# A state space layer as a scan pipeline over feature chunks, with its turn table and read-out operators made one stage earlier

## The chip, the cores and the metric

The kernel runs on one core of a Trainium2 chip. The metric is the device time of one execution in microseconds. TensorE (PE) multiplies matrices, with its weight loads (PEld) beside it; VectorE (DVE), ScalarE (ACT) and GpSimd (POOL) work on tiles in SBUF and read TensorE's results from PSUM; SyncE (SP) and the other queues issue transfers. Each engine runs its instructions in the order in which they stand in its queue.

## The reference

Two transformer blocks on 512 tokens of 1024 features in float32: a retention and pooling mixer, a mixture of 32 experts, a gated input, then a state space layer, a gated feed-forward net, a short convolution and a second feed-forward net. The change concerns the state space layer and the stage before it:

```python
h = h + sigmoid(rms_norm(h) @ ple_gate_w) * (p @ ple_proj_w)   # gated input
# state space layer: 64 groups of 16 features, 64 complex states each
lr, li, dt = minimum(a_re, -1e-4), a_im, exp(log_step)
abar = exp(lr * dt) * (cos(li * dt) + 1j * sin(li * dt))
u = modulate(rms_norm(x, norm1_g), sh1, sc1)                   # (512, 64 groups, 16)
state[t] = abar * state[t - 1] + bbar @ u[t]                   # by group, complex
y = real(c @ state) + d * u
val, gate = split(gelu(y) @ ssm_w_out)
x = x + g1 * val * sigmoid(gate)
```

## The kernel before

The program runs stage by stage: mixer, router and experts, `stage_ple` (gated input), `stage_s5` (state space layer), then feed-forward, convolution and feed-forward. A scheduler and tile pools turn the code into one queue of instructions per engine; tiles with one tag share slots, and an instruction that wants a slot waits until the slot's last readers are done. A product in float32 is done as three in a reduced format: a weight block is loaded (`raw`, `half`), ScalarE makes its high part (`wh`, L94), VectorE the rest (`wl`, L95), and TensorE multiplies three times (L115 to L117).

`stage_ple` multiplies the normalised input by `ple_gate`. The token factors come from a power on GpSimd (`lrstd`, L229), which TensorE spreads over the partitions (`bc`, L241). Each of the eight output blocks c is then evacuated: VectorE scales the product (`lg`, L1343), ScalarE takes the sigmoid (L1344), VectorE multiplies by the projected input `pj` (L1345), adds to `res` (L1346), and two sums of squares `lacc` collect on ScalarE and VectorE (L204, L220). Beside it run the last columns of a modulation vector: `halves` loads six `half` tiles on GpSimd's queue, VectorE reduces each (`adaj`, L1077). At the end GpSimd takes the roots `r2` (L1369) and `r1`.

`stage_s5` cuts the 512 tokens into 64 chunks of 8 steps. For each of eight feature chunks k it normalises (`zh`), regroups (`zt`, `zct`, `zu`, `zU`), and multiplies with operators made earlier (`s_pt`) to get the input that each chunk of 8 steps adds to the states (`zs`). The recurrence over the 64 chunks then runs on VectorE for all features at once, in two halves, one step after the other:

```python
nc.vector.tensor_tensor(t[:, j, :, :, :2], a8, x[:, c - 1]..., ALU.mult)              # L1518
net.scanned = nc.vector.tensor_reduce(x[:, c], t[:, j], AX.X, ALU.add).ins             # L1520
```

Here `a8` holds the complex factor of eight steps. ScalarE copies the states into `zxq` (L1524). TensorE adds the part within the chunks (`zy<-zT,zU`, L1562, all eight k before the recurrence is done) and the part from the states (`zy<-zQ,zxq`, L1573), turns the result back to features (`zf`, L1583); ScalarE applies the gelu (L1586), and ScalarE, VectorE and GpSimd split it in two (`zgah`, `zgal`, L1589 to L1592) for the output layer `ssm_out`, whose first product is `mm<-zgah,wh` (L146).

The read-out operators `zQ` are made in `readout`, called inside `stage_s5` and issued behind `r2`: sixteen times three products on GpSimd (L1117, L1119, L1121, tile `ro`), each written to DRAM (`q_d`) and loaded back by SyncE.

Of the kernel before, what the change touches and what calls it, by code (L numbers as in the profile page):

```python
# [22 lines left out]
S = 512  # L23
# [19 lines left out]
EXTRA = 0  # L43
NA = 5
ZK = (0, 5, NK)
# [468 lines left out]
def stage_mix_out(net, mixed, ps, moe):  # L514

    nc, a = net.nc, net.a
    with ExitStack() as es:
        net.h1 = net.h1p.tile([128, NT, D], F32, tag="big", name="h1")
        router = Router(net, es, moe)
        moe.prefetch(6)  # L520
# [12 lines left out]
        moe.prefetch(9)  # L533
# [243 lines left out]
class Moe:  # L777
# [30 lines left out]
    def prefetch(self, n):  # L808

        net = self.net  # L810
        while len(self.loaded) < n:
            j = len(self.loaded)
            nm, e, b = self.order[j]
            src = net.a[nm][e][b]
            q = j % (9 + EXTRA)
            if q < 6:
                t = net.load(src, self.raw2, "raw2")
            else:
                t = net.load(src) if q < 9 else net.load(src, self.raw3, "raw3")
            self.loaded.append(t)  # L820
# [76 lines left out]
    def experts(self, es):  # L897
# [6 lines left out]
        if EXTRA:  # L904
            self.raw3 = pool("raw3", EXTRA)
# [12 lines left out]

# [190 lines left out]
def powers4(t):  # L1109
    return t.rearrange("p (g t h) -> p g t h", g=GP, t=8)  # L1110


def power_product(eng, out, t, xr, xi, y1, y2, op):

    sh = [128, GP, 8, 16]
# [8 lines left out]
class S5Prepare:  # L1124


    def __init__(self, net, p1, pt):
# [5 lines left out]
        net.a8 = net.rt.tile([128, 2, G // 2, 2], F32, name="a8")  # L1133
# [4 lines left out]
    def units(self):  # L1138
# [24 lines left out]
        for b in range(2):  # L1163
# [8 lines left out]
            sincos(net, ang, ei, lam, t[:, :256], t[:, 256:])  # L1172
            tt(ei, er, ei, ALU.mult)
# [6 lines left out]

        for h in range(2):
            r = slice(64 * h, 64 * h + 64)
            for q in range(2):
                nc.vector.tensor_copy(net.a8[r, q, :, q], ar[r, 8, h::2])
            nc.vector.tensor_scalar(net.a8[r, 0, :, 1], ai[r, 8, h::2], -1.0, None, op0=ALU.mult)
            nc.vector.tensor_copy(net.a8[r, 1, :, 0], ai[r, 8, h::2])
# [83 lines left out]
def stage_ple(net):  # L1270
# [3 lines left out]
    with ExitStack() as es:  # L1274
# [22 lines left out]
        net.linear_fm(a["ple_proj"], 2, lambda k: pact[k], evac_p)  # L1297
        first = [net.load(a["ple_gate"][b]) for b in range(2)]
# [52 lines left out]
        for z in range(2):  # L1351
            t = net.op.tile([128, 32, 128], F32, tag="op", name=f"s_pt{z}")
            for q in range(2):
                o = slice((2 * z + q) * 2048, (2 * z + q + 1) * 2048)
                with tc.issue_after(copied[-1]):
                    nc.scalar.dma_start(t[:, 16 * q:16 * q + 16].rearrange("p g x -> p (g x)"), net.p_d[:, o])
# [60 lines left out]
def readout(net):  # L1417

    nc, a = net.nc, net.a
    e, w = [net.whp.tile([128, 2048], F32, tag="wh", name=f"ro{j}") for j in range(2)]  # L1420
# [506 lines left out]
```

## Time and profile before

| what | value |
|---|---|
| median of 3 runs | 2694.6 us (2694.42 to 2696.72) |
| profiled execution | 2704.24 us, its span 2701.8 us |
| TensorE busy | 2558.8 us, 95% of the span |
| VectorE busy | 1898.3 us, 70% |
| ScalarE busy | 1374.8 us, 51% |
| GpSimd busy | 430.1 us, 16% |
| granted TensorE clock, mean | 0.97 |

Busy shares are means over stages that differ; the windows among the rows below cut the span into stages. A row of a timeline gives the start in us from the span's beginning, the duration (of all that it groups, with x and their count), the engine, the line and the operation (out<-in), and in brackets the idle time before it and what ended that. A row of windows gives the engines in the order PE, PEld, DVE, ACT, POOL, with the number of instructions in brackets.

### The profile page before, as it was taken

The numbers are of one execution on the slowest core, as the hardware profiler recorded it, in microseconds if no ns is written. First come the engines' busy times: TensorE is split into PE (matmuls) and PEld (weight loads), VectorE is DVE, ScalarE is ACT, GpSimd is POOL, SyncE is SP. The second block draws the span as 40 slices with busy tenths as digits, with TensorE's granted clock in tenths as the row PEclk, the third lists the DMA queues.
The fourth block names the chain that finished last, engine by engine and source line by source line (L and its number), as shares of the span: only waits on it lengthen the run. The fifth ranks groups of instructions, "written<-read, shape, count | busy, mean of one in ns | idle before, by whom it ended". The sixth has DMA issues, their size and how long they took to land.

```text
span 2701.8 us, 31654 instructions
## 1 busy us (share of the span) xinstructions
PE 2558.8 (95%) x12270; PEld 1927.6 (71%) x12271; DVE 1898.3 (70%) x2410; ACT 1374.8 (51%) x1513; POOL 430.1 (16%) x252
## 2 busy tenths in 40 slices
PE   8999788999999999999999865999999999999998
PEld 6767555666666666666666755888788888888886
DVE  8974877999999999898988577775553544532333
ACT  7344565777777777777776644242122322322221
POOL 3362312031312112031200071000000000000000
PEclk9999898999999999999999987999999999999999
DMA  6435788999999999999996642754552222223221
GB/s 210 172 110 214 292 289 305 355 341 383 346 383 356 373 360 375 352 358 373 368 372 239 248 150 80 278 188 177 210 214 104 103 97 103 83 86 103 101 85 63
DMA packets 110432, 634.76 MB, mean 235 GB/s; under 512 B 16043, under 2 KB 21419, under 8 KB 43331
## 3 DMA queue, kind: packets, MB, share of 16 engines
q1 hardware_dynamic: 97971, 599.69, 59.6%
q0 software_dynamic: 11584, 28.27, 4.2%
q10 hardware_dynamic: 720, 4.72, 0.4%
q8 instruction: 98, 1.61, 0.2%
q14 instruction: 59, 0.48, 0.1%
HBM read 607.15 MB, written 28.61 MB: 235 GB/s over the span
## 4 chain that ended last, share of the span: by engine, by line
PE 66%; issue 18%; DMA 7%; DVE 6%; POOL 2%; ACT 2%; SPq 0%; POOLq 0%; DVEq 0%; ACTq 0%
PE gu L115 8%; PE gu L116 8%; PE gu L117 8%; PE mm L115 7%; PE mm L116 7%; PE mm L117 7%; PE dn L116 4%; PE dn L117 4%; PE dn L115 4%; DMA xg<-hn_d,tabim 2%; DMA acc_d<-y,tabim 2%; DMA raw<-in_w_ada 1%; PE mm L146 1%; DVE wl L95 1%; PE mm L147 1%
## 5 line engine op out<-in xcount | busy, mean ns | idle before, releaser
L95 DVE TENSOR_TENSOR el<-raw,eh 128x2048 fp32r<-128x2048 f32 (+1 forms) x396 | 874.5, 2221 | 99.3 <-ACT eh L94 93.2
L94 ACT ACTIVATE eh<-raw 128x2048 fp32r<-128x2048 f32 (+1 forms) x396 | 735.2, 1866 | 294.0 <-PE gu L117 209.9
L94 ACT ACTIVATE wh<-raw 128x1024 fp32r<-128x1024 f32 (+1 forms) x238 | 222.0, 981 | 478.2 <-PE mm L116 291.9
L116 PE MATMUL gu<-el,xh 128*88 128x512 f32 x1024 | 404.2, 395 | 0.0
L117 PE MATMUL gu<-eh,xl 128*88 128x512 f32 x1024 | 402.4, 393 | 0.0
L115 PE MATMUL gu<-eh,xh 128*88 128x512 f32 x1024 | 400.6, 397 | 0.0
L95 DVE TENSOR_TENSOR wl<-raw,wh 128x1024 fp32r<-128x1024 f32 (+1 forms) x238 | 265.5, 1148 | 79.9 <-ACT wh L94 79.6
L116 PE MATMUL mm<-nl,wh 128*128 128x512 f32 x816 | 318.3, 390 | 0.0
L115 PE MATMUL mm<-nh,wh 128*128 128x512 f32 x816 | 317.9, 390 | 0.0
L117 PE MATMUL mm<-nh,wl 128*128 128x512 f32 x816 | 316.8, 389 | 0.0
L117 PEld LDWEIGHTS gu<-eh,xl 128*88 128x88 f32 x1024 | 158.4, 155 | 78.4 <-issue 0.5
L116 PEld LDWEIGHTS gu<-el,xh 128*88 128x88 f32 x1024 | 158.9, 155 | 75.8 <-issue 0.5
L115 PEld LDWEIGHTS gu<-eh,xh 128*88 128x88 f32 x1024 | 158.3, 155 | 75.3 <-issue 0.3
L115 PE MATMUL dn<-eh,ath 128*88 128x512 f32 x512 | 204.0, 401 | 0.4
L116 PE MATMUL dn<-el,ath 128*88 128x512 f32 x512 | 202.5, 399 | 0.0
L117 PE MATMUL dn<-eh,atl 128*88 128x512 f32 x512 | 202.4, 396 | 0.0
L750 POOL DMA_INDIRECT acc_d<-y,tabim x32 | 93.8, 2931 | 633.0 <-ACT y L958 566.1
L744 POOL DMA_INDIRECT xg<-hn_d,tabim x32 | 142.2, 4444 | 318.9 <-PE xt L758 157.4
L115 PEld LDWEIGHTS mm<-nh,wh 128*128 128x128 f32 x816 | 153.2, 188 | 32.7
L117 PEld LDWEIGHTS mm<-nh,wl 128*128 128x128 f32 x816 | 153.2, 188 | 32.3
L116 PEld LDWEIGHTS mm<-nl,wh 128*128 128x128 f32 x816 | 153.2, 188 | 31.5
L1681 DVE TENSOR_TENSOR fs<-fs,mm 128x512 f32<-128x512 f32 x44 | 30.2, 687 | 205.8 <-PE mm L117 196.4
(468 smaller groups left out, 3925.7 us busy)
## 6 DMA issues: line engine op xcount, KB each, us to landing
raw<-in_w_gu SPq DMA_DIRECT2D x256, 1024.0 KB, 8.7
raw<-in_w_down SPq DMA_DIRECT2D x128, 1024.0 KB, 7.5
raw<-in_w_ada SPq DMA_DIRECT2D x45, 1024.0 KB, 4.9
raw<-in_w_ffn_in SPq DMA_DIRECT2D x44, 1024.0 KB, 4.8
raw<-in_w_ffn_out SPq DMA_DIRECT2D x32, 704.0 KB, 4.1
raw<-in_conv_in SPq DMA_DIRECT2D x12, 1024.0 KB, 4.9
raw<-in_ssm_out SPq DMA_DIRECT2D x8, 1024.0 KB, 5.0
raw<-in_w_out SPq DMA_DIRECT2D x4, 1024.0 KB, 4.8
```

The source lines that it names most:

```text
L94: nc.scalar.activation(h, x, AF.Copy)
L95: nc.vector.tensor_tensor(l, x, h.bitcast(F32), ALU.subtract)
L115: mm(ps, sh, mh, start=start, stop=False)
L116: mm(ps, sh, ml, start=False, stop=False)
L117: return mm(ps, sl, mh, start=False, stop=stop).ins
L146: self.nc.tensor.matmul(ps[c], wh, ah, start=k == 0, stop=False)
L147: self.nc.tensor.matmul(ps[c], wl, ah, start=False, stop=False)
L744: return net.nc.gpsimd.indirect_dma_start(out=dst, out_offset=None, in_=net.hn_d[:, :], in_offset=bass.IndirectOffsetOnAxis(ap=idx, axis=0 ...
L750: net.nc.gpsimd.indirect_dma_start(out=net.acc_d[:, :], out_offset=bass.IndirectOffsetOnAxis(ap=idx, axis=0), in_=src, in_offset=None, com ...
L1681: nc.vector.tensor_tensor(t, t, ps, ALU.mult)
```

## The change

The recurrence is no longer stepped. The states of a feature chunk are turned by the angle that their factor has gathered up to each chunk position, which leaves a real factor; one scan instruction of VectorE over 128x512 runs the real recurrence (L1562 in the new file), and the result is turned back. The eight feature chunks run as a pipeline: chunk n is normalised while n-2 is scanned, n-4 read out and n-5 turned to features.

For this a table of cosines and sines by chunk position is needed. `s5_turns` makes it on VectorE in `stage_ple` (tiles `tu_w`, `tu_c0`, `tu_c1`; 42 small products and sums, 24 of 128x512) from `turn`, which takes the place of `a8`; GpSimd writes it to DRAM (`r_d`), and SyncE loads it in `stage_s5` (`ztab`, 2 MB). `s5_readout` does the work of `readout` in `stage_ple`: the 48 products on GpSimd, with all their transfers on GpSimd's queue (4 loads of `e_d`, 8 of `c1` and `c2`, 16 writes of `q_d`, 2 of `r_d`, 1 MB each). The four `s_pt` loads of 1 MB take slots of the same pool as the table, so that each waits for a slot. The shared work pool goes from two tiles of 16 KB a partition to four of 8 KB. The split after the gelu goes to ScalarE and GpSimd alone; all `zct` copies go to ScalarE.

```diff
@@ stage_ple
         net.linear_fm(a["ple_proj"], 2, lambda k: pact[k], evac_p)
+        room, turns = s5_turns(net)
         first = [net.load(a["ple_gate"][b]) for b in range(2)]
...
             net.step(99)
+        s5_readout(net, room, turns)
...
-        for z in range(2):
-            t = net.op.tile([128, 32, 128], F32, tag="op", name=f"s_pt{z}")
...
+        for z in range(4):
+            t = net.op.tile([128, 16, 128], F32, tag="op", name=f"s_pt{z}")
+            with tc.issue_after(copied[-1]):
+                nc.scalar.dma_start(t.rearrange("p g x -> p (g x)"), net.p_d[:, z * 2048:(z + 1) * 2048])
@@ new functions
+def s5_turns(net):
...
+    def times(o, x, y, t):
+        for r, op in ((0, ALU.subtract), (1, ALU.add)):
+            vec.tensor_tensor(o[r], x[0], y[r], ALU.mult)
+            vec.tensor_tensor(t, x[1], y[1 - r], ALU.mult)
+            vec.tensor_tensor(o[r], o[r], t, op)
...
+    for b in range(4):
...
+        times([ov[:, r] for r in range(2)], [v[:, m].unsqueeze(3).to_broadcast(sh) for v in hi],
+              [v[:, m].unsqueeze(2).to_broadcast(sh) for v in lo],
+              scratch.rearrange("p (m a b) -> p m a b", m=M, a=8))
+    return w[:, 1536:], c
+def s5_readout(net, room, turns):
...
+    for q in range(G // GP):
...
+        if q % 4 == 0:
+            gp.dma_start(c1, a["s_c1"][:, 64 * q:64 * q + 256])
+            gp.dma_start(c2, a["s_c2"][:, 64 * q:64 * q + 256])
+            gp.tensor_scalar(c1, c1, net.sign, -1.0, op0=ALU.mult, op1=ALU.mult)
...
+        power_product(gp, t, f[:, 1024:1536], er[:, :, g], ei[:, :, g], y1, y2, ALU.subtract)
+        gp.dma_start(net.q_d[:, q * 512:(q + 1) * 512], t)
+        if q == 2:
+            for j in range(2):
+                gp.dma_start(net.r_d[:, 2048 * j:2048 * j + 2048], turns[j])
@@ stage_s5
+            def turned(x, sign):
+                w = [p2.tile(sh, F32, tag=f"zw{j}", name=f"zw{k}_{sign}_{j}") for j in range(2)]
+                tt(w[0], x, cos.unsqueeze(2).to_broadcast(sh), ALU.mult)
+                for r in range(2):
+                    if (r == 0) == (sign > 0):
+                        tt(w[1][:, :, r], x[:, :, 1 - r], sin, ALU.mult)
+                    else:
+                        nc.vector.scalar_tensor_tensor(w[1][:, :, r], x[:, :, 1 - r], -1.0, sin, ALU.mult, ALU.mult)
+                return w
+            w = turned(pv, 1)
+            nc.gpsimd.tensor_tensor(w[0], w[0], w[1], ALU.add)
+            x = p2.tile(sh, F32, tag="zx", name=f"zx{k}", bufs=2)
+            nc.vector.tensor_tensor_scan(x.rearrange(flat), ro.rearrange(flat), w[0].rearrange(flat), 0.0, ALU.mult, ALU.add)
+            w = turned(x, -1)
...
+                    (nc.gpsimd if h == r else nc.vector).tensor_tensor(
+                        xq[64 * r:64 * r + 64, h, :, 1:], w[0][i, :, r, :NCH - 1], w[1][i, :, r, :NCH - 1], ALU.add)
...
-        with tc.high_priority(offset=-1000), tc.issue_after(net.rooted):
-            readout(net)
...
+        for n in range(NK + 6):
...
+            stage(norm, 0)
+            stage(to_chunks, 0)
+            stage(to_groups, 1)
+            stage(states, 2)
+            stage(scan, 2)
+            stage(outputs, 4)
...
+            stage(to_features, 5)
```

GpSimd's queue around the root `lrstd`, in the kernel before: the six loads of `half`, then the two roots, then the read-out.

```order
L1325 DMA half_1_13131<-in_w_ada 128x1024
L1325 DMA half_0_13137<-in_w_ada 128x1024
L1325 DMA half_1_13138<-in_w_ada 128x1024
L229 TENSOR_TENSOR lrstd<-rs_13148,half 128x4
L1369 TENSOR_TENSOR r_13495<-lv_13496,half 128x4
```

The same place now, behind the first three `half` loads and the loads of `c1` and `c2`. Tile `ro_f` holds the read-out's factors and results, `tu_w` its powers.

```order
L1465 TENSOR_SCALAR ro_f<-ro_f,consts 128x256
L1111 TENSOR_TENSOR ro_f<-tu_w,ro_f 128x512
L1109 TENSOR_TENSOR ro_f<-tu_w,ro_f 128x512 x2
L1113 TENSOR_TENSOR ro_f<-ro_f 128x512
L1470 DMA q_d<-ro_f 128x512
L1111 TENSOR_TENSOR ro_f<-tu_w,ro_f 128x512
L1317 DMA half_1_13205<-in_w_ada 128x1024
L1317 DMA half_0_13211<-in_w_ada 128x1024
L1113 TENSOR_TENSOR ro_f<-ro_f 128x512
L1109 TENSOR_TENSOR ro_f<-tu_w,ro_f 128x512
L1317 DMA half_1_13212<-in_w_ada 128x1024
L227 TENSOR_TENSOR lrstd<-rs_13305,half 128x4
```

The last three `half` loads and `lrstd` moved behind the start of the read-out; 20 more of its products, two scalings and 15 transfers stand between `lrstd` and `r2`, and the remaining 21 products stand among the stage's own work on GpSimd.

VectorE's queue at the first evacuations `lg`, before.

```order
L1077 SCALAR_TENSOR_TENSOR adaj_13122,mods_77<-half_1_13131,adac_12950 128x1024
L95 TENSOR_TENSOR wl_13321<-raw_13318,wh_13320 128x1024
L1080 TENSOR_TENSOR mods_77<-mods_77,consts 128x2
L95 TENSOR_TENSOR wl_13321<-raw_13318,wh_13320 128x1024
L1343 TENSOR_TENSOR lg_13222<-mm_13166,lrb 128x512
L1343 TENSOR_TENSOR lg_13229<-mm_13167,lrb 128x512
L1077 SCALAR_TENSOR_TENSOR adaj_13122,mods_77<-half_0_13137,adac_12950 128x1024
```

The same place now, with the table's products (`tu_w`, `tu_c`) in it.

```order
L1069 SCALAR_TENSOR_TENSOR adaj_13196,mods_77<-half_0_13211,adac_12949 128x1024
L1420 TENSOR_TENSOR tu_w<-tu_w 128x512
L93 TENSOR_TENSOR wl_13480<-raw_13477,wh_13479 128x1024 x2
L1421 TENSOR_TENSOR tu_c_13074<-tu_c_13074,tu_w 128x8x64
L1069 SCALAR_TENSOR_TENSOR adaj_13196,mods_77<-half_1_13212,adac_12949 128x1024
L1336 TENSOR_TENSOR lg_13381<-mm_13325,lrb 128x512
L1336 TENSOR_TENSOR lg_13388<-mm_13326,lrb 128x512
```

The evacuations of the first two blocks moved behind the last two `adaj`; before they stood ahead of them.

VectorE's queue in the state space stage now, one turn of the loop from the additions of chunk 0 to the forward turn of chunk 2 (`zw` are turned states, `zx` the scan's result, `zxq` the states for the read-out).

```order
L1569 TENSOR_TENSOR zxq_13829<-zw_-1_0_13824,zw_-1_1_13825 64x4x63 x2
L1562 SCALAR_TENSOR_TENSOR zx_13886<-zrho_13683,zw_1_0_13880 128x512
L1550 TENSOR_TENSOR zw_-1_0_13888<-zx_13886,ztab 128x512
L1555 SCALAR_TENSOR_TENSOR zw_-1_1_13889<-zx_13886,ztab 128x4x64
L1553 TENSOR_TENSOR zw_-1_1_13889<-zx_13886,ztab 128x4x64
L1550 TENSOR_TENSOR zw_1_0_13944<-zs_13926,ztab 128x512
L1553 TENSOR_TENSOR zw_1_1_13945<-zs_13926,ztab 128x4x64
L1555 SCALAR_TENSOR_TENSOR zw_1_1_13945<-zs_13926,ztab 128x4x64
```

These nine instructions for each of eight chunks stand where 62 steps of four instructions stood.

## Rows read from the trace of the kernel before

**Rows 1.** The page, busy time: us, share of the span, instructions.

```profile
PE 2558.8 (95%) x12270; PEld 1927.6 (71%) x12271; DVE 1898.3 (70%) x2410; ACT 1374.8 (51%) x1513; POOL 430.1 (16%) x252
```

**Rows 2.** Windows by stage: from:to, length, engines' busy us, clock, DMA share, GB/s.

```profile
1566.00:1585.00 19.00, 17.41 (x253) 14.95 (x254) 8.19 (x12) 16.10 (x24) 18.51 (x21) 0.84 0.46 155
1585.00:1649.00 64.00, 15.67 (x265) 14.60 (x263) 61.55 (x225) 26.86 (x63) 38.63 (x34) 0.67 0.30 108
1649.00:1678.00 29.00, 28.28 (x387) 27.18 (x388) 13.07 (x34) 18.52 (x33) 5.66 (x5) 0.91 0.35 126
1678.00:1740.00 62.00, 62.00 (x269) 49.95 (x268) 56.51 (x96) 19.79 (x24) 0.00 (x0) 1.00 0.74 277
```

**Rows 3.** Timeline of TensorE, state space stage.

```profile
1568.55 3.63 PE L1472 MATMUL zt<-consts,zh 128*64 128x128 f32 x16 [1.59 <-ACT zh L1464]
...
1572.75 1.09 PE L1472 MATMUL zt<-consts,zh 128*64 128x128 f32 x8
...
1649.72 6.51 PE L1573 MATMUL zy<-zQ,zxq 128*64 128x128 f32 x56 [46.82 <-issue]
1656.16 3.40 PE L1583 MATMUL zf<-consts,zyt 64*64 64x64 f32 x64
...
1678.07 0.48 PE L146 MATMUL mm<-zgah,wh 128*128 128x512 f32 x1
```

**Rows 4.** Timeline of GpSimd, gated-input stage.

```profile
1504.62 1.72 POOL L1325 DMA_DIRECT2D half<-in_w_ada  x3
...
1522.04 1.08 POOL L229 TENSOR_TENSOR lrstd<-rs,half 128x4 f32<-128x4 f32 x1
1564.77 1.02 POOL L1369 TENSOR_TENSOR r<-lv,half 128x4 f32<-128x4 f32 x1 [41.65 <-DVE lv L1368]
```

**Rows 5.** Tile half: time from issue to landing.

```profile
DMA to landing us min/median/max: 8.6/9.2/14.2
```

**Rows 6.** DMA issues, 1500 to 1690: KB each, median us to landing.

```profile
s_pt<-p_d ACTq DMA_DIRECT2D x4, 1024.0 KB, 12.5
...
zQ<-q_d SPq DMA_DIRECT2D x4, 1024.0 KB, 4.8
```

**Rows 7.** Groups by form, GpSimd and ScalarE in the stage: busy us, mean ns.

```profile
L1121 POOL TENSOR_TENSOR ro<-ro 128x512 f32<-128x512 f32 x16 | 20.4, 1275 | 0.7
...
L1117 POOL TENSOR_TENSOR ro<-ro 128x512 f32<-128x512 f32 x16 | 17.7, 1108 | 4.5 <-DMA q_d<-ro 4.4
...
L1586 ACT ACTIVATE zg<-zf 128x512 f32<-128x512 f32 x8 | 4.7, 597 | 5.0 <-PE zf L1583 5.0
```

**Rows 8.** Timeline of VectorE, gated-input stage.

```profile
1503.26 2.36 DVE L95 TENSOR_TENSOR wl<-raw,wh 128x1024 fp32r<-128x1024 f32 x2 [17.57 <-ACT wh L94]
...
1523.76 1.23 DVE L1077 SCALAR_TENSOR_TENSOR adaj<-half,adac 128x1024 bf16<-128x1024 f32 x1 [2.48 <-DMA half<-in_w_ada]
...
1527.26 1.28 DVE L1343 TENSOR_TENSOR lg<-mm,lrb 128x512 f32<-128x512 f32 x2
...
1559.76 0.69 DVE L1346 TENSOR_TENSOR res<-res,lg 128x512 f32<-128x512 f32 x1
...
1567.00 1.40 DVE L1463 SCALAR_TENSOR_TENSOR zh<-res,gainf,bc 128x512 f32<-128x512 f32 x2 [2.31 <-PE bc L241]
```

**Rows 9.** Timelines, VectorE and GpSimd at 98 to 106, VectorE at 1598 to 1634.

```profile
103.64 2.30 DVE L1077 SCALAR_TENSOR_TENSOR adaj<-raw,adac 128x1024 bf16<-128x1024 f32 x1
...
98.76 2.10 POOL L1119 TENSOR_TENSOR s_tp<-s_ai,s_bc 128x512 f32<-128x512 f32 x1
...
1601.51 1.89 DVE L1518 TENSOR_TENSOR zr<-a,zX 128x80 f32<-128x80 f32 x2
...
1630.92 0.35 DVE L1518 TENSOR_TENSOR zr<-a,zX 128x80 f32<-128x80 f32 x2
```

**Rows 10.** Windows by granted clock, first half of the state space stage.

```profile
1569.00:1573.00 4.00, 4.00 (x25) 3.13 (x24) 3.48 (x6) 3.36 (x6) 4.00 (x4) 0.62 0.84 258
1573.00:1602.00 29.00, 26.77 (x480) 24.83 (x480) 17.29 (x38) 22.98 (x39) 24.61 (x23) 1.00 0.35 124
```

More of the change, by code (lines that the diff above doesn't have):

```diff
@@ L1172, in units @@
             sincos(net, ang, ei, lam, t[:, :256], t[:, 256:])
+            if b:
+                for h in range(2):
+                    r = slice(64 * h, 64 * h + 64)
+                    for j, v in enumerate((ar[r, 8, h::2], lam[r, 3 * G + h::2], ai[r, 8, h::2])):
+                        nc.vector.tensor_copy(net.turn[r, j], v)
             tt(ei, er, ei, ALU.mult)
@@ L1456, in stage_s5 @@
         rb = net.bcast_tok(net.r2)
-        U = [p1.tile([128, HG, NCH], F32, name=f"zU{z}") for z in range(2)]
-        X = [p1.tile([128, NCH, 2, 4 * (ZK[z + 1] - ZK[z])], F32, name=f"zX{z}") for z in range(2)]
-        XQ, hts, cts = {}, {}, {}
+        tab = p1.tile([128, G // 2, 2, NCH], F32, name="ztab")
+        tv = tab.rearrange("p m r c -> p (m r c)")
+        rho = [p1.tile([128, 4, 2, NCH], F32, name=f"zrho{j}") for j in range(2)]
+        for j in range(2):
+            nc.gpsimd.memset(rho[j][:, :, :, 0], 0.0)
+        U, XQ, hts, cts, sts = {}, {}, {}, {}, {}
         def norm(k):
@@ L1587, in to_features @@
                                  AF.Gelu_apprx_tanh)
[L1588 to L1592 removed]
+            if k % 2 == 0:
+                g = op.tile([128, 2, 2, S], F32R, tag="op", name=f"zga{k}")
+                ga[k], ga[k + 1] = [(g[:, 0, j], g[:, 1, j]) for j in range(2)]
@@ L1594, in stage_s5 @@
+            h, l = ga[k]
+            nc.scalar.activation(h, t, AF.Copy)
+            nc.gpsimd.tensor_tensor(l, t, h.bitcast(F32), ALU.subtract)
+        for j in range(2):
+            nc.sync.dma_start(tv[:, 2048 * j:2048 * j + 2048], net.r_d[:, 2048 * j:2048 * j + 2048])
         load_t(0)
+        load_q(0)
         load_t(2)
-        with tc.high_priority(offset=-1000), tc.issue_after(net.rooted):
-            readout(net)
-        for k in range(NK):
-            norm(k)
-        scans = []
@@ L1617, in stage_s5, with stage @@
-        for x in scans:
-            list(x)
-        gah = op.tile([128, NK, S], F32R, tag="op", name="zgah")
-        gal = op.tile([128, NK, S], F32R, tag="op", name="zgal")
+        load_q(2)
         load_t(4)
         load_t(6)
-        for k in range(NK):
-            within(k)
-        for k in range(0, NK, 2):
-            load_q(k)
-        for k in range(NK + 1):
-            if k < NK:
-                outputs(k)
-            if k:
-                to_features(k - 1)
+        for n in range(NK + 6):
+            def stage(f, lag):
+                if 0 <= n - lag < NK:
+                    f(n - lag)
+            stage(norm, 0)
[4 more added lines that the diff above has]
+            stage(outputs, 4)
+            if n in (5, 7):
+                load_q(n - 1)
+            stage(to_features, 5)
```

200 lines of the change are left out of this document (79 added, 121 removed).

## The prediction

> **What bounds the kernel now.** The page comes first: TensorE is busy for 95% of the span [rows 1], so in nearly all of it only TensorE's own work counts, and a change that touches other engines can pay only where TensorE stands still. Cutting the span into stages [rows 2] shows where that is: the state space stage (1566 to 1678) holds most of the missing time, with TensorE busy 15.67 of 64 us between 1585 and 1649, while VectorE is busy 61.55 of those 64. Its place is plain: on TensorE's timeline [rows 3] the read-out product zy starts at 1649.72 after 46.82 us idle, since it waits for the step-by-step recurrence on VectorE (62 steps in two halves, products L1518, sums L1520). From 1678 on TensorE is busy 62.00 of 62 us [rows 2]. So the first product of the output layer, at 1678.07 [rows 3], is the clock on the wall: what this change moves it by, the end moves by. Before the stage stands another chain that decides: GpSimd takes the root lrstd at 1522.04 and the root r (r2) at 1564.77, and sits idle between them [rows 4]; TensorE waits for both, since each is spread by TensorE (bc) before anything behind it can go on.
>
> **What the change removes.** All recurrence steps and their copies on ScalarE. With them goes the 46.8 us wait, if what replaces them runs alongside TensorE. TensorE's own work in the stage is 17.41 + 15.67 + 28.28 = 61.4 us [rows 2], so the stage's 113.3 us (1564.77 to 1678.07) cannot shrink by more than about 45, with the way in (10 us) kept.
>
> **What it adds ahead of the stage.** Three things are late there.
>
> First, lrstd. In GpSimd's order the loads of c1 and c2, a scaling, seven products and four DMA issues now stand ahead of it. The three half loads ahead of c1 leave by 1506.3 [rows 4] and take 8.6 to 14.2 us [rows 5], so c1 and c2, behind them in one queue, are there at 1516 to 1521; I take 1520. The scaling costs less than a product, I take 0.7; seven products are 5 x 1.11 + 2 x 1.27 = 8.1 [rows 7], four issues 4 x 0.57 = 2.3, by the three that took 1.72 [rows 4]. lrstd then starts at 1531, and with VectorE's table products in between at 1532 to 1533: 10 us late.
>
> Second, the first evacuation lg. Before, it came at 1527.26 [rows 8]. Now it stands behind all six adaj on VectorE, and the last half load is issued only just before lrstd, at 1531; 9.2 us [rows 5] and one adaj (1.23 [rows 8]) later it is 1541.5, and the table's last products share the stretch. I take 1546, 19 us late. TensorE's banks are full meanwhile.
>
> Third, the pace of the evacuations. VectorE has from there 24 lg and res operations and 14 sums lacc at 0.69 [rows 8], six table products and one pair wl: about 33 us of its own work, as long as before (1527.3 to 1560.5). But 38 of these read both inputs from SBUF while GpSimd multiplies, and the rows show what that costs: a VectorE product (adaj) of 1.23 us alone [rows 8] took 2.30 beside GpSimd, GpSimd's product of 1.11 [rows 7] took 2.10, and a pair of recurrence steps went from 0.35 to 1.89 [rows 9]. Each waits for the other's instruction to end. The norm zh, with one operand in PSUM, took 1.40 for two beside GpSimd's products: no wait. Between lrstd and r2 GpSimd has 20 products, 15 DMA issues and two scalings, 20 x 1.16 + 15 x 0.57 + 1.4 = 33 us of its own; about ten products are left at 1546, and each holds up one VectorE operation by 1.16: 12 us. The end comes at 1546 + 33 + 12 = 1591 less the 2 us that ScalarE's waits and these overlap, 1589, and r2 at 1593 instead of 1564.77: **28 us late**. The s_pt loads, which ScalarE now issues only behind the landing of r_d, stall its queue but end inside this time (12.5 us each [rows 6], the second at about 1573).
>
> The table itself costs little: nine of its large products and the small ones fall into VectorE's idle 17.57 us before 1503.26 [rows 8] (42 small at about 0.2, by the 0.35 for two of 80 elements [rows 9], nine at 0.69: 15 us). Without that cover it would be 15.
>
> **The stage itself.** From r2 to the first scan: before, r2 to the norm takes 2.2 us and zs of the first chunk follows about 10 us after r2 (eight zt at 1572.75 stand just ahead of it [rows 3]); then the forward turn (one product of 512 and two of 256, 0.69 + 2 x 0.35 = 1.4) and GpSimd's sum 1.27 with one read-out product ahead of it: 15 us. The first scan starts at 1608. The table ztab waits for q4 to q7, whose writes now end at about 1588, and needs 3 MB of transfer behind them in three loads (zQ, of 1 MB like each of these, landed after 4.8 us [rows 6]): 1604 where the queue is free, just in time, and up to 8 us later where it isn't.
>
> Per chunk VectorE has: forward 1.4, scan, back 1.4, two additions 0.7. The trace shows no scan. Its lower bound is the 0.69 of a two-input operation over 512 elements, its upper 1.23 (the longest operation on VectorE near here, adaj [rows 8]); it is nearest to the first, which I take. VectorE: 4.2 us. GpSimd has 1.27 for the sum, 2 x 0.6 for its two additions, 1.27 for zga, 0.1 of memset, and over six chunks the rest of the read-out that is queued in between: 15 products and nine issues, 15 x 1.16 + 9 x 0.57 = 22.5, or 3.8 a chunk. Together 7.7. Of VectorE's nine operations six have both inputs in SBUF, 3 us; if half of them hold up GpSimd the chunk takes 9.2, if all 10.7, if none 7.7. TensorE's chunk is 61.4 / 8 = 7.7, so GpSimd and VectorE set the pace. I take 9.6, as back turn and additions always meet queued products: six times 9.6, one last chunk at 6, and 2.4 for a weight pair wl that stands on VectorE between chunks 4 and 5: 66 us. Scan 7 starts at 1674. Behind it: scan and back turn 2.1, additions 1.3, zy 1.9 (6.51 for 56 of them, 16 a chunk), its copy 0.6, zf 1.7 (3.40 for 64, 32 a chunk) [rows 3], gelu [rows 7] and split 0.6 each, in all 8.8, and I take 9.5 us with what is queued on ScalarE: the first output product at 1683.5 instead of 1678.07.
>
> [...] No row here shows a scan, so the sum stays with 0.69.
>
> **Sum.** +28 at r2; stage 1593 to 1683.5, 90.5 us instead of 113.3, -23; together **+5.5 us**. The profiled execution took 2704.24 (span 2701.8 and 2.4 around it), 9.6 more than the median 2694.6; I put the difference on the median: 2694.6 + 5.5 = 2700.
>
> **Rivals.**
> *The shared waits hardly count (faster).* If GpSimd's and VectorE's instructions overlap freely here, r2 comes 12 us earlier (no held-up evacuations) at 1581, and the chunk takes 7.7: 1581 + 15 + 6 x 7.7 + 6 + 2.4 + 9.5 = 1660, 18 us ahead of before: 2677. For it: in most of the recurrence GpSimd's products took their plain 1.11 on the mean [rows 7]. Against it: VectorE's then did not (1.89 for 0.35, [rows 9]). The point from which it decides: a chunk of 8.5 us together with r2 before 1588 already brings a gain.
> *Nothing measurable.* The two sides cancel to 5 us: a chunk of 9 instead of 9.6 takes 3.6 off the sum and leaves +2, 2696; for that only one more in ten of the shared waits has to fall away.
> *TensorE's clock falls in the stage (slower still).* Where 0.62 of the clock was granted, sixteen zt took 3.63 us, at 1.00 eight took 1.09 [rows 3, 10]: 1.7 times. Before, the mean was 0.67 from 1585 to 1649, where TensorE mostly stood idle [rows 2]. If it falls for half of the chunks, TensorE's chunk of 7.7 becomes 13 and passes the 9.6: 4 x 3.4 = 14 more, 2714. For it: the loop leaves TensorE idle for 2 us of each 9.6, and lrstd stalls it for 10 us ahead of the stage. Against it: from 1573 to 1602, where TensorE worked for 26.77 of 29 us on the same short products, it was granted 1.00 [rows 10]. Dearer DMA issues on GpSimd (36 instead of 6; e_d goes in pieces of 128 bytes) end on the same side: at 0.9 each, 24 x 0.36 = 9 us on GpSimd's queue, of which 3 to 5 reach the end.
> *The change doesn't shorten the stage.* If the loop waits on r_d, ztab or s_pt by 10 us more, r2's delay stands alone: 2710. I count it with the last.
>
> **How the numbers follow.** Main case (+1 to +11) 0.42; the shared waits hardly count 0.23; cancelled 0.17; clock or queue 0.18. A measurement tells some 0.2% from no change, 5.4 us. The main case lies half on either side of this line, so: slower 0.18 + 0.26 = 0.44; within 0.2% 0.16 + 0.10 = 0.26; faster 0.23 with a part of the cancelled case, 0.30. The range leaves out the extremes of both outer cases: 2674 to 2714; the likeliest case alone is 2696 to 2706.
>
> **What would show it.** In the changed profile: lrstd at 1531 to 1534, the first lg near 1546, VectorE's L1338 and L1339 near 1.5 instead of 0.69 while GpSimd multiplies, r2 at 1588 to 1597, zy without its long idle, scans L1562 every 9 to 10 us and the last at 1670 to 1678, the first product of the output layer near 1683. The prediction is wrong if r2 comes before 1580, if chunks follow at 7.7 or less, if a scan costs well over 1.2, or if the stage runs at the lower clock.

## The result, and the profile of the changed kernel

The changed kernel takes 2731.65 us (median of 4 runs, 2729.04 to 2734.65), the kernel before 2694.53: a ratio of 1.0136 [1.0119, 1.0154]. The forecast was 2700 with a range of 2674 to 2714, so the time lies outside the range. The profiled execution took 2734.65 us, its span 2731.9, against 2704.24 and 2701.8 before.

First the steps that the prediction named. The timeline of GpSimd in the gated-input stage answers to [rows 4]:

```profile
1517.06 0.99 POOL L1465 TENSOR_SCALAR ro_f<-ro_f,consts 128x256 f32<-128x256 f32 x1 [8.41 <-DMA ro_f<-in_s_c]
...
1530.48 1.07 POOL L227 TENSOR_TENSOR lrstd<-rs,half 128x4 f32<-128x4 f32 x1
...
1553.26 0.58 POOL L1473 DMA_DIRECT2D r_d<-tu_c  x1 [9.21 <-DVE tu_c L1421]
...
1562.48 1.11 POOL L1111 TENSOR_TENSOR ro_f<-tu_w,ro_f 128x512 f32<-128x512 f32 x1
1563.67 1.64 POOL L1113 TENSOR_TENSOR ro_f<-ro_f 128x512 f32<-128x512 f32 x1
...
1591.40 1.05 POOL L1360 TENSOR_TENSOR r<-lv,half 128x4 f32<-128x4 f32 x1 [6.71 <-DVE lv L1359]
```

`lrstd` starts at 1530.48 instead of 1522.04 and `r2` at 1591.40 instead of 1564.77: 26.6 us late. The two idle times are those of the order: 8.41 us until c1 and c2 have landed, 9.21 us until VectorE has the second part of the table. VectorE's timeline in the same stage and in the scan loop, beside [rows 8, 9]:

```profile
1543.64 1.28 DVE L1336 TENSOR_TENSOR lg<-mm,lrb 128x512 f32<-128x512 f32 x2
...
1547.39 0.68 DVE L1339 TENSOR_TENSOR res<-res,lg 128x512 f32<-128x512 f32 x1
...
1562.14 2.01 DVE L1339 TENSOR_TENSOR res<-res,lg 128x512 f32<-128x512 f32 x1
1564.08 0.68 DVE L1336 TENSOR_TENSOR lg<-mm,lrb 128x512 f32<-128x512 f32 x1
...
1605.28 1.23 DVE L1562 TENSOR_TENSOR_SCAN zx<-zrho,zw 128x512 f32<-128x512 f32 x1 [0.80 <-POOL zw L1559]
...
1614.68 2.69 DVE L1562 TENSOR_TENSOR_SCAN zx<-zrho,zw 128x512 f32<-128x512 f32 x1 [1.57 <-POOL zw L1559]
...
1669.65 2.18 DVE L1562 TENSOR_TENSOR_SCAN zx<-zrho,zw 128x512 f32<-128x512 f32 x1
```

The first `lg` comes at 1543.64 instead of 1527.26. A product that reads both inputs from SBUF takes 0.68 us while GpSimd stands still (1547.39) and 2.01 beside its product of 1562.48; `lg`, with one input in PSUM, keeps 0.68 beside the one of 1563.67. The scan takes 1.22 us at its shortest (1662.82, 1.23 at 1605.28) and up to 2.69 beside GpSimd's products. TensorE's waits from 1490 to 1760 (what waits, for what: us in total, times, longest):

```profile
PE ts L210 <- DVE lacc L218: 16.5, 1, 16.5
PE zy L1606 <- DVE zxq L1569: 10.6, 5, 3.8
PE bc L239 <- POOL lrstd L227: 7.8, 1, 7.8
```

The 46.82 us of [rows 3] are gone; TensorE now waits 16.5 us ahead of the stage (`ts`, the sums behind the last `lacc`), 7.8 at `lrstd` and 10.6 in the loop. TensorE's timeline where the stage ends:

```profile
1662.94 1.55 PE L1606 MATMUL zy<-zQ,zxq 128*64 128x128 f32 x16 [1.84 <-DVE zxq L1569]
1665.16 1.90 PE L1618 MATMUL zf<-consts,zyt 64*64 64x64 f32 x32 [0.67 <-ACT zyt L1609]
...
1675.08 2.85 PE L1606 MATMUL zy<-zQ,zxq 128*64 128x128 f32 x16 [3.81 <-DVE zxq L1569]
1677.86 5.99 PE L1618 MATMUL zf<-consts,zyt 64*64 64x64 f32 x64
...
1684.54 0.77 PE L144 MATMUL mm<-zga,wh 128*128 128x512 f32 x1
...
1688.04 0.39 PE L144 MATMUL mm<-zga,wh 128*128 128x512 f32 x1
```

The first product of `ssm_out` starts at 1684.54, 6.5 us later than before. The forecast of this moment was 1683.5. Up to here the change does what was said. But the span grew by 30.1 us, so 23.6 us more are lost *behind* it, where both kernels run the same products. Windows of both kernels from that product to the end of the span, cut at the first product of the convolution and at that of the second net, so that the first holds `ssm_out` and the first net (columns as in [rows 2]). Before:

```profile
1678.07:2146.15 468.08, 463.16 (x2044) 380.52 (x2041) 270.09 (x415) 133.49 (x175) 3.23 (x4) 1.00 0.50 182
2146.15:2328.91 182.76, 181.97 (x805) 149.28 (x805) 89.65 (x118) 50.68 (x65) 1.01 (x1) 1.00 0.27 92
2328.91:2701.80 372.89, 362.29 (x1604) 299.95 (x1604) 134.28 (x163) 98.94 (x133) 1.01 (x1) 0.99 0.25 88
```

After:

```profile
1684.54:2163.55 479.01, 473.69 (x2042) 383.04 (x2040) 267.38 (x410) 131.20 (x173) 4.48 (x5) 0.99 0.49 178
2163.55:2349.69 186.14, 185.35 (x804) 149.43 (x804) 89.62 (x118) 50.72 (x65) 1.01 (x1) 1.00 0.25 91
2349.69:2731.90 382.21, 371.18 (x1604) 300.91 (x1604) 134.22 (x163) 98.91 (x133) 1.01 (x1) 0.99 0.24 86
```

The same work (2044 and 2042 recorded instructions of TensorE, 805 and 804, 1604 and 1604, nearly all of them 128x512 products) takes 479.01 instead of 468.08 us, 186.14 instead of 182.76, 382.21 instead of 372.89, and TensorE is the busy engine in all six windows: 10.9 + 3.4 + 9.3 = 23.6. It isn't waiting more, it is slower per product. The clock explains little of it: 1.00 or 0.99 in all six. The groups of TensorE over the whole run (count | busy us, mean ns of one) say the same of one of the products of these stages, here of before and then of after:

```profile
L117 PE MATMUL mm<-nh,wl 128*128 128x512 f32 x816 | 316.8, 389 | 0.0
```

```profile
L115 PE MATMUL mm<-nh,wl 128*128 128x512 f32 x816 | 321.4, 395 | 0.0
```

A full-speed window of the second net, where TensorE does nothing else, gives the pace without any wait, before (with one of the convolution) and after:

```profile
2200.00:2300.00 100.00, 100.00 (x438) 82.04 (x438) 44.32 (x56) 25.14 (x31) 0.00 (x0) 1.00 0.27 95
2400.00:2600.00 200.00, 200.00 (x884) 165.62 (x883) 66.42 (x76) 52.29 (x68) 0.00 (x0) 1.00 0.27 95
```

```profile
2420.00:2620.00 200.00, 200.00 (x862) 162.16 (x861) 63.57 (x74) 49.79 (x65) 0.00 (x0) 1.00 0.28 96
```

862 products fit where 884 did: 2.5%. From one start to the next on the timeline (gaps of 0.3 us and more left out) it is 0.2267 us before and 0.2324 after in both nets, 0.2289 and 0.2333 in the convolution.

### The profile page after: what moved, and what is told of

It is laid out like the page before. It is cut to its first block, busy times and chain, and to the rows that moved or that the text cites. A ratio compares the mean times of both kernels' runs of the same rounds, so it can differ in the third digit from the quotient of the medians.

```text
span 2731.9 us, 31540 instructions
## 1 busy us (share of the span) xinstructions
PE 2595.9 (95%) x12270; PEld 1940.1 (71%) x12271; DVE 1928.5 (71%) x2292; ACT 1354.1 (50%) x1465; POOL 489.2 (18%) x318
```

## The experiments

What could change the pace of products whose instructions are the same? In the compiled programs one thing differs for them, the addresses of what they stream: `turn` takes 384 bytes a partition where `a8` took 512, and the tiles that are placed later lie 128 bytes lower; the weights `wh` and `wl`, placed early, don't move. Addresses within a partition, modulo 512:

```
tiles                         before   after   weights (both)
ffn 0 and 1: nh, nl, fh, fl      320     192   320
convolution: nh, nl, ch, cl      384     256   320
ssm_out: zgah, zgal; zga          32     416   320
gate: lhh                        480     480   320
```

The distance below is the streamed tile's address less that of the weights, modulo 512.

**Theory:** the pace depends on where the streamed tile lies relative to the weights. **Rival:** it is the new code (other engines' traffic, the clock, another order), and the address is chance. Four kernels tell these apart. All comparisons are with the kernel before on the same chip.

**e1: the place alone is put back.** The tile gets its 128 bytes again, unused.

```diff
-        net.turn = net.rt.tile([128, 3, G // 2], F32, name="turn")
+        net.turn = net.rt.tile([128, 4, G // 2], F32, name="turn")
```

> The changed kernel with its turn tile made 128 bytes a partition longer, so that every tile placed after it lies where it lay in the kernel before. In the changed profile the first output product came only 6.5 us late, and the other 24 us of the loss built up evenly over the feed-forward and convolution stages, whose instructions are the same: a product followed the last after 0.232 us instead of 0.227. Theory (place of the tiles in memory): turn is 128 bytes shorter than a8, and this shift costs TensorE its pace; the pace returns to 0.227 in both feed-forward stages, and the time falls by 20 to 25 us to some 2709. Rival (the stages run slower for another reason, such as what the new state space stage leaves behind in queues and prefetches): the pace stays at 0.232 and the time at 2731.

2699.78 us (2695.47 to 2707.84, 7 runs) against 2696.78: 1.0018 [1.0004, 1.0032]. Window of the second net:

```profile
2400.00:2600.00 200.00, 200.00 (x884) 165.61 (x883) 66.44 (x76) 52.33 (x68) 0.00 (x0) 1.00 0.28 94
```

884 products again. The 128 unused bytes take 1.2% off the changed kernel, and what the change itself does is left: +0.18%, 4.9 us (by the interval 1.1 to 8.6), where the forecast was 5.5. The time is 9 us below the 2709 expected for this run; not all of that is explained (see Left open).

**e2: the place alone, in the kernel before.** 384 unused bytes ahead of the pools of both nets and the convolution, with one small memset each.

```diff
+        if PADS[2 * layer]:
+            pad = es.enter_context(tc.tile_pool(name=f"fpad{layer}", bufs=1, reuse_waits="tile"))
+            nc.gpsimd.memset(pad.tile([128, PADS[2 * layer] // 4], F32, name=f"fpad{layer}")[:, :1], 0.0)
```

> The kernel before, with 384 unused bytes a partition ahead of each of the feed-forward and convolution stages, which moves their tiles to the same remainder of 512 bytes as in the changed kernel, and nothing else. Theory (place of the tiles): 0.232 us from product to product instead of 0.227 in the feed-forward stages, and 20 us more, some 2715. Rival (something of the new state space stage): no change, 2694 to 2696.

2717.16 us (2715.11 to 2721.55, 4 runs): 1.0080 [1.0064, 1.0097], 21.6 us, with not one instruction of the change.

```profile
2400.00:2600.00 200.00, 200.00 (x863) 162.16 (x862) 65.76 (x75) 50.79 (x68) 0.00 (x0) 1.00 0.27 94
```

863 products. The rival falls with this run: the old code at the new place has the new pace.

**e3: each stage gets another stage's place.** As e2, with 64 bytes ahead of the first net, 448 ahead of the convolution, 128 ahead of the second net.

```diff
-PADS = (384, 384, 384)
+PADS = (64, 448, 128)
```

> The kernel before, with 64 unused bytes ahead of the first feed-forward stage, 448 ahead of the convolution, 128 ahead of the second feed-forward stage: tiles at remainders 384, 320 and 448 of 512. If the place decides and not the stage, the convolution takes the 0.227 us that the feed-forward stages had at 320, and the first feed-forward stage the 0.229 that the convolution had at 384; 448 is not known. If the stage decides, the paces stay 0.227, 0.229 and 0.227.

2707.05 us (one run). The convolution's and the second net's windows:

```profile
2200.00:2300.00 100.00, 100.00 (x443) 82.78 (x442) 45.80 (x59) 25.21 (x31) 0.00 (x0) 1.00 0.28 96
2400.00:2600.00 200.00, 200.00 (x862) 162.17 (x861) 65.76 (x76) 51.74 (x67) 0.00 (x0) 1.00 0.26 91
```

The convolution, now at the weights' own remainder (320), does 443 in 100 us where it did 438; the second net, 128 above it, falls to 862. Start to start the convolution has 0.2267 us and the first net, 64 above the weights, 0.2289: the two have changed places. The time fits too: 3.5 us for the first net, -1.8 for the convolution and 9.1 for the second net make 10.8, and the run is 10.3 above the median of before. It is the place, not the stage.

**e4: everything moves together.** An early tile is 128 bytes larger, so the weights and the streamed tiles of the nets, the convolution and `ssm_out` all lie 128 higher.

```diff
-        self.onec = c.tile([128, 1], F32, name="onec")
+        self.onec = c.tile([128, 33], F32, name="onec")[:, :1]
```

> The kernel before, with 128 more bytes a partition ahead of all tiles from the constants on, so that weights and activations move together. If what counts is how the activations lie relative to the weights, the pace stays 0.227 in the feed-forward stages and the time some 2695; if the absolute place of the activations counts, it is that of remainder 448, the same as in the second feed-forward stage of the run with single shifts.

2694.74 us (one run), and the old pace:

```profile
2400.00:2600.00 200.00, 200.00 (x884) 165.68 (x883) 65.72 (x75) 52.33 (x68) 0.00 (x0) 1.00 0.27 94
```

So the address alone does not decide; the distance does. Strictly, it is the distance to what is placed early: the weights are the one part of it that these products read, but they were not moved alone. The gate comes nearest to that. Its tiles are placed from the other end and stay at 480 while the weights move to 448, and its products take 1 ns less each on the mean (395 to 397 ns, by line, instead of 396 to 398).

The next runs start from e1 and ask what holds the stage itself. Since the stages ahead end at times that differ by some us from one execution to the next (the first `half` load was issued at 1498.4 to 1507.6 in these profiles), moments are given from that load on. On this scale the first product of `ssm_out` comes at +173.5 in the kernel before, +178.6 in the changed one and +175.8 in e1. One profile is good to some 3 us here: e2, e3 and e4 run the code of before up to this point and have +170.6 to +170.9, and the changed kernel and e1 run the same code. In the runs that follow, the tiles lie where e1 has them, in the last two apart from what their edits move.

**e5: `lrstd` ahead of the read-out.** GpSimd takes the root first and then 47 of the 48 products; one stays ahead of it.

```diff
-        s5_readout(net, room, turns)
...
-        net.rsqrt(rstd, ssq, 1.0 / D, 1e-5)
+        root = net.rsqrt(rstd, ssq, 1.0 / D, 1e-5)
+        s5_readout(net, room, turns, root)
...
+            with net.tc.issue_after(root):
+                gp.tensor_scalar(c1, c1, net.sign, -1.0, op0=ALU.mult, op1=ALU.mult)
```

> The changed kernel with its tiles back in place (turn 128 bytes longer, as in all runs from here on but the last), and the read-out's products (but one) and lrstd exchanged on GpSimd: lrstd ahead. Theory (the queue on GpSimd and the shared waits set r2): lrstd at 1522 to 1525 instead of 1530.5, the first lg at about 1536 instead of 1543.6, r2 some 5 to 8 us earlier than 1591.4, and the time lower by as much than the 2700 of the version with the tiles back. Rival (the evacuations are held up by the products in any case, so that GpSimd's later products only press more on them): r2 within 2 us of 1591, no gain.

2712.81 us (2709.7 to 2716.3, 5 runs) against 2695.86: 1.0063 [1.0042, 1.0084], slower than e1. GpSimd's timeline and one of TensorE's waits:

```profile
1514.66 1.08 POOL L227 TENSOR_TENSOR lrstd<-rs,half 128x4 f32<-128x4 f32 x1
...
1580.01 1.05 POOL L1360 TENSOR_TENSOR r<-lv,half 128x4 f32<-128x4 f32 x1 [6.06 <-DVE lv L1359]
```

```profile
PE zy L1607 <- DMA zQ<-q_d: 16.3, 1, 16.3
```

`r2` comes at +80.0, 6 us earlier than in e1 (+86.1), but the first product at +186.3 instead of +175.8. All that GpSimd did behind the root it has to do later: the last of the 16 operators is written at 1668 and TensorE waits 16.3 us for it. The read-out's length on GpSimd is a bound of its own, which an earlier root doesn't move.

**e6: the scan writes to PSUM.** Its result overwrites the product that it came from, so the turn back reads one operand from PSUM. (VectorE and ScalarE read PSUM in these kernels; no instruction of GpSimd does, though the opening names it with them. Its tiles stay in SBUF.)

```diff
-            x = p2.tile(sh, F32, tag="zx", name=f"zx{k}", bufs=2)
+            x = pv
```

> Tiles back in place, and the scan writes its result into the PSUM bank that the states came in, so that the three turn-back operations of each chunk have one operand in PSUM instead of two in SBUF. Theory (VectorE and GpSimd wait for each other's whole instruction where VectorE reads two operands from SBUF): turn-back at 0.7 and 0.4 us with no waits, where it now takes up to 1.76 and 1.49; the chunks follow in 8.0 to 8.5 us instead of 9.2, and the time falls by 5 to 9 us. Rival (GpSimd's own queue sets the pace, 7.7 us a chunk and in-order waits): chunks as before, within 2 us of 2700.

2699.71 us (2695.3 to 2704.93, 10 runs): 1.0014 [1.0001, 1.0026]; first product at +172.0, 3.8 us ahead of e1. VectorE's timeline:

```profile
1604.88 1.23 DVE L1562 TENSOR_TENSOR_SCAN zs<-zrho,zw 128x512 f32<-128x512 f32 x1 [0.74 <-POOL zw L1559]
1606.14 0.69 DVE L1550 TENSOR_TENSOR zw_-1_0_13823<-zs,ztab 128x512 f32<-128x512 f32 x1
```

The turn back takes its plain 0.69 (1.42 at this place in the changed kernel), in all eight chunks, and the scans follow each other in 8.6 us instead of 9.2; 8.0 to 8.5 had been expected. The gain forecast for the total is not seen: the ratio is e1's within the intervals.

**e7: the evacuations stay in PSUM.** `lg` is written back over the product.

```diff
-            t = p6.tile([128, S], F32, tag="t2", name=f"lg{c}")
+            t = ps
```

> Tiles back in place, and the gate of the input stage computed in its PSUM bank: lg, sigmoid and the product with pj in place, so that 16 of the operations L1338 and L1339 have one operand in PSUM. Theory (shared waits stretch the evacuations by about 12 us): L1338 and L1339 at 0.7 us beside GpSimd's products, r2 5 to 8 us earlier, the time lower by as much. Rival (TensorE sets the pace here, or ScalarE's queue behind the s_pt loads): r2 within 2 us of 1591.

2702.22 us (2698.23 to 2710.16, 10 runs): 1.0022 [1.0009, 1.0035]. VectorE's groups in the stage (the line's eight instructions: busy us, mean ns) and TensorE's waits:

```profile
L1338 DVE TENSOR_TENSOR mm<-mm,pj 128x512 f32<-128x512 f32 x8 | 5.5, 685 | 0.6 <-ACT mm L1337 0.6
...
L1339 DVE TENSOR_TENSOR res<-res,mm 128x512 f32<-128x512 f32 x8 | 5.4, 677 | 0.1
```

```profile
PE zy L1606 <- DVE zxq L1569: 15.2, 5, 6.8
PE ts L210 <- DVE lacc L218: 8.9, 1, 8.9
```

The products fall to 0.68 us on the mean (1.05 and 1.18 in the changed kernel) and `r2` comes at +78.2, 8 us ahead of e1, as forecast. The time doesn't follow: against the changed kernel the wait for `ts` falls from 16.5 to 8.9, and that for `zxq` in the loop grows from 10.6 to 15.2. In the profile the last scan (+157.8) is 7 us ahead of e1 and the first product (+172.4) 3.4.

**e8: e5, e6 and e7 together.**

> The last three edits together. If they act on different stretches of the same chain, their gains add: 15 to 22 us below the version with the tiles back, 2678 to 2685, below both kernels. If GpSimd's total of work between lrstd and the last chunk is the bound, the sum is well short of that: some 8 us.

2700.74 us (2696.18 to 2708.64, 10 runs): 1.0015 [0.9999, 1.0031]. `r2` at +74.0 and the last scan at +153.6 are the earliest so far, and yet the first product comes at +176.6. A window of the loop and one wait of TensorE:

```profile
1600.00:1650.00 50.00, 38.06 (x533) 35.11 (x534) 40.07 (x54) 23.77 (x35) 48.71 (x52) 0.89 0.25 90
```

```profile
PE zy L1607 <- DMA zQ<-q_d: 18.4, 1, 18.4
```

GpSimd is busy for 48.71 of 50 us, with the time in it by which its products are stretched (one product of `ro_f` takes 2.02 us at 1606.00, one of the same kind 1.12 at 1608.57), and TensorE's longest wait is for operators that it writes: it has become the bound. The gains don't add, and even the 8 us of the second expectation are not there.

**e9: the read-out's inputs earlier.** From e1: the first c1 and c2 are loaded ahead of the `half` loads, and the table is written behind the fourth and seventh operator, so that GpSimd should wait for neither.

```diff
+    with net.tc.high_priority(offset=1000):
+        gp.dma_start(f[:, 1536:1792], a["s_c1"][:, :256])
+        cload = gp.dma_start(f[:, 1792:], a["s_c2"][:, :256]).ins
...
-        if q == 2:
-            for j in range(2):
+        if q in (3, 6):
+            j = q // 6
+            with net.tc.issue_after(done):
```

> Tiles back in place; the loads of the first c1 and c2 ahead of the half loads on GpSimd's queue, so that the read-out starts when lgate lets the queue go on instead of at c1's landing 11 us after the first half load, and the second write of r_d four chunks of the read-out later, so that GpSimd doesn't stand 9.2 us behind the table. Theory (the read-out's total of work on GpSimd, from its start to the last chunk, sets the end of the stage): about 18 us of GpSimd's idle time go, and 6 to 15 us of them reach the end: 2685 to 2694. Rival (the stage is set by r2 and the shared waits): r2 within 3 us of before relative to the first half load, 2698 to 2702.

2701.93 us (2700.67 to 2706.93, 11 runs) against 2696.86: 1.0024 [1.0013, 1.0034]. No gain. GpSimd's root:

```profile
1526.05 1.44 POOL L227 TENSOR_TENSOR lrstd<-rs,half 128x4 f32<-128x4 f32 x1
```

At +20.2 it is 3.8 us ahead of e1, `r2`, at +81.6, 4.5, and the last scan, at +160.6, 4.4; at the first product (+176.6) nothing is left. It is lost behind the last scan, not in the loop. Windows from the last scan to the first product, of e1 and of e9:

```profile
1663.40:1674.17 10.77, 9.03 (x119) 8.46 (x118) 8.81 (x10) 3.87 (x7) 3.29 (x4) 0.88 0.15 52
```

```profile
1666.49:1682.47 15.98, 13.05 (x118) 12.19 (x117) 7.74 (x10) 4.22 (x7) 5.20 (x4) 0.61 0.19 67
```

The same products take 5 us more: TensorE has a granted clock of 0.61 instead of 0.88, and VectorE waits 1.74 us and makes a pair `wl` (2.36 us) before it turns the last chunk back. The waits of GpSimd are not all gone either: that for the table's second part is 4.85 us where it was 9.21.

**e10: e9 with e6 and e7.**

> The last edit with the scan's result and the gate in PSUM. Theory (total of work on GpSimd): with the start early, fewer shared waits now reach the end: another 6 to 10 us, 2678 to 2688. Rival: no more than the early loads alone.

2691.28 us (2684.99 to 2699.34, 12 runs): 0.9987 [0.9977, 0.9998]. TensorE's waits:

```profile
PE zy L1621 <- DVE zxq L1584: 10.7, 4, 5.9
PE ts L210 <- DVE lacc L218: 7.1, 1, 7.1
```

10.7 us below e9, against an expected 6 to 10; the 2678 to 2688 forecast from e9's expected time is missed. First product at +167.2, 8.6 us ahead of e1. With fewer shared waits in both stages and an earlier start of the read-out together, a gain reaches the end. e6 and e7 together without the early loads were not run, so it isn't shown that these are needed.

**e11: e10 with the places of the gate and the convolution set.** 160 and 448 unused bytes bring their streamed tiles to the weights' remainder.

```diff
+        lpad = es.enter_context(tc.tile_pool(name="lpad", bufs=1, side="right", reuse_waits="tile"))
+        nc.gpsimd.memset(lpad.tile([128, 40], F32, name="lpad")[:, :1], 0.0)
...
+        cpad = es.enter_context(tc.tile_pool(name="cpad", bufs=1, reuse_waits="tile"))
+        nc.gpsimd.memset(cpad.tile([128, 112], F32, name="cpad")[:, :1], 0.0)
```

> The last version, with 160 unused bytes ahead of the gate's input tiles and 448 ahead of the convolution's, so that both lie at the remainder 320 of 512, as the weights do. Theory (place): 0.227 us from product to product in the gate's product (0.234 now) and in the convolution (0.229), some 3 us less. Rival (the gate's product is paced by its evacuations): only the 1.7 us of the convolution.

2689.26 us (2681.52 to 2696.95, 11 runs): 0.9970 [0.9958, 0.9982], faster than both kernels. The convolution's window:

```profile
2200.00:2300.00 100.00, 100.00 (x443) 82.81 (x442) 44.94 (x57) 25.86 (x32) 0.00 (x0) 1.00 0.27 95
```

443 products in 100 us, as in e3; start to start the gate falls from 0.2343 to 0.2271 us, the convolution from 0.2289 to 0.2267. The paces are as the theory has them; that the total gains some 3 us over e10 is not clear of the noise, as the intervals of the two overlap.

**e12: e11 with every second `zga` subtraction on VectorE.**

```diff
-            nc.gpsimd.tensor_tensor(l, t, h.bitcast(F32), ALU.subtract)
+            (nc.vector if k % 2 else nc.gpsimd).tensor_tensor(l, t, h.bitcast(F32), ALU.subtract)
```

> The last version, with the second part of the split after the gelu on VectorE for the odd chunks, 5 us less on GpSimd and 2.7 more on VectorE. If GpSimd's total sets the end, 2 to 4 us less; if the loop on VectorE does, 1 to 3 us more.

2694.29 us (2688.52 to 2697.99, 11 runs): 0.9992 [0.9983, 1.0001]. The expected gain is not there: the median is 5.0 us above e11's, and the intervals of the two just part (0.9983 and 0.9982). That is the way of the second expectation, and more than its 1 to 3 us. But the profiled execution was nearly the fastest, 2688.75, and in it the first product comes at +163.4, 2.4 us ahead of e11, so where the time goes isn't shown.

## Why the prediction was wrong

**The step that failed** is the one about the clock on the wall: "what this change moves it by, the end moves by". It took TensorE's pace behind 1678 as given because the work there is the same and TensorE is busy for 62.00 of 62 us. But busy is not pace. The change made a tile 128 bytes smaller, all later tiles moved by that, and each product of the two nets takes 2.5% longer, of the convolution 1.9%. e2 shows the cause with no other edit, e1 the reverse, e4 that it is a distance and not an address. The sizes fit: 1604 products x 0.0057 = 9.1 us for each net (9.3 measured in the second), 805 x 0.0044 = 3.5 for the convolution (3.4). Of the 10.9 us in `ssm_out` and the first net about 1.5 are the lower clock at 1684: from the first start to the ninth it is 3.50 us, at a granted clock of 0.51, before 1.94 at 1.00.

**The rest of the sum held**, partly by luck, as errors cancelled:

- *`lrstd`*: 1531 forecast with 1532 to 1533 taken, 1530.48 measured; *first `lg`*: 1546, 1543.64; *`r2`*: 1593, 1591.40. Behind `lrstd` two errors cancel: c1 and c2 let GpSimd go on at 1517.06 and not at 1520, and the seven products took 10.1 us and not 8.1. The cause at the evacuations is the one named: VectorE's products with two inputs in SBUF are held up beside GpSimd's (1.05 and 1.18 us on the mean at L1338 and L1339, 0.68 alone). e7 confirms it by taking the cause away: 0.68 on the mean with one operand in PSUM.
- *Table and first scan*: 1608 forecast, 1605.28. The table `ztab` cost no wait of its own.
- *The scan* was mis-sized: 0.69 taken, 1.23 measured, the upper end and 1.8 times 0.69.
- *The chunk*: 9.6 forecast, with a shorter last one 66 us from the first scan to the eighth; 64.4 measured, from 1605.28 to 1669.65, or 9.2 each. As the scan alone was at least 0.54 us dearer, the rest of a chunk was cheaper than taken; which part of it was not worked out.
- *Behind the last scan*: 9.5 us forecast from its neighbours, 14.9 measured. 32 `zf` took 1.90 us at a granted clock of 1.00, the last 64 took 5.99, and sixteen `zy` 2.85 instead of 1.55: by these rows 2.2 + 1.3 = 3.5 us of it is the clock, and 1.5 is the scan itself (2.18 for 0.69). TensorE had stood still for 3.81 us before those `zy`. This is the rival of the falling clock, in part: it came in the chunk at 1651.77 (behind 4.23 us of standing still) and at the end (granted clock 0.57 and 0.50), while from 1605 to 1646 it was 1.00.
- *+5.5 us in all*: e1, which holds the change without its new addresses, has +4.9, with an interval of 1.1 to 8.6, so that the agreement to 0.6 us is luck.
- *The working* has three slips that don't move the result: the main case's 0.42 is said to lie half on either side of the line, but is split 0.26 and 0.16; a chunk shorter by 0.6 us takes two in ten of its 3 us of shared waits, not one; and 0.9 for a DMA issue is 0.33 above the 0.57 taken, not 0.36.

The windows that show the clock are those of the chunk at 1651.77, of the end of the stage and of the first eight products behind it:

```profile
1651.77:1662.00 10.23, 8.65 (x64) 7.89 (x64) 10.13 (x11) 2.26 (x4) 8.48 (x8) 0.57 0.37 128
1675.08:1684.54 9.46, 9.46 (x84) 9.01 (x85) 3.39 (x4) 2.41 (x4) 1.26 (x1) 0.50 0.30 113
1684.54:1688.04 3.50, 3.50 (x11) 2.78 (x10) 3.11 (x5) 0.63 (x1) 1.28 (x1) 0.51 0.00 0
```

**The rivals.** That the shared waits hardly count is refuted by 2.01 us for 0.68, by `r2` at 1591.40 instead of its 1581 and by chunks 9.2 apart instead of 7.7. Dearer DMA issues: 0.53 to 0.63 us each, with 0.96 for the e_d loads, as that rival had it; but only two of the issues between `lrstd` and `r2` are of that kind. No rival had the place in it.

Of e5 to e9 each eased one bound and another took its place: the shared waits, GpSimd's own length, the stretch behind the last scan with its falling clock. Only where several were eased without delaying the read-out, in e10, did the total gain.

**Left open.** The medians are 37.1 us apart, the two profiles 30.4. The profile of before was an execution 9.7 us above its median, that of after one 3.0 above; e1 against after differs by 32 us in the times, while their profiles from the first product to the end differ by 24. Of the rest those two profiles show 7.6 us ahead of the first `half` load, where executions of one kernel differ by some us, and 2.8 from there to the first product; whether the changed kernel has a part of its own there was not tried. The tiles of the mixer moved by 128 bytes too, but there the effects nearly cancel: where its tile `hnh` is streamed past the weights, 48 products fall from a median of 398 ns to 388, and where `hnh` takes the part of the weights, 64 rise from 388 to 396. Nor was it tried why the distance matters.

## What to carry to other kernels

When unchanged work takes another time, compare the pace of one unchanged instruction in a stretch without waits: here TensorE was busy for 200.00 of 200 us in both kernels, with 884 products in the one and 862 in the other. A tile that got 128 bytes smaller moved the tiles placed behind it, so look at the distance between streamed tiles and weights before judging an edit by its time. And an engine that was freed from one wait took on the next (in e5 `r2` came 6 us earlier, and TensorE then waited 16.3 us for operators): count the total length of what is queued on the helper engine before putting more there or starting it later.

## What the runs showed of the hardware

The pace of products of 128x512 in the reduced format at a granted clock of 1.00, each with a weight load of 128 columns beside it, by the distance of streamed tile and weights (start to start, gaps left out):

```
distance, bytes mod 512   us       where
  0                       0.2267   nets before and e1; convolution e3, e11; gate e11 (0.2271)
 64                       0.2289   convolution before and e1; first net e3
128                       0.2324   second net e3
160                       0.2343   gate, before and after
384                       0.2324   nets after and e2
448                       0.2333   convolution after and e2
```

Distances of 96 and 224 (`ssm_out`, after and before) both have 0.2333. Each row stands for the stages and runs named; why the distances order so is not shown. In a kernel with TensorE busy for 95% of the span these 2 to 3% are larger than all that the change did on purpose. The second point is how VectorE and GpSimd hold each other up: one product of VectorE takes 0.68 us with GpSimd idle and 2.01 beside its product, and 0.69 and 0.68 in e6 and e7 once one operand is in PSUM. One product of GpSimd takes 1.11 us at 1562.48 and up to 2.94 beside VectorE's (1553.86). At the start of the loop the ends alternate: the scan ends at 1606.51, GpSimd's product of 1605.78 at 1607.40 after 1.62 us, VectorE's of 1606.54 at 1607.96 after 1.42, and GpSimd's of 1607.37 at 1608.92 after 1.55. Each of these three products ends 0.56 to 0.96 us behind what ended before it on the other engine; the shortest of their lines are 0.69 (L1550), 1.11 (L1111) and 1.10 (L1109).
